# Second block: rotated queries summed in PSUM, key copies and sums of squares on the scalar engine

## The chip, the cores and the metric

One NeuronCore of one Trainium2 chip runs the whole program. The metric is device time in microseconds (us) of one execution; lower is better. The engines are named as in the profile: PE is TensorE (PEld its weight loads), DVE is VectorE, ACT is the scalar engine, POOL is GpSimd, and SP is the engine whose queue issues the large weight loads.

## What is computed

The program runs two transformer blocks over 256 tokens of width 1024. The first (gated linear attention, retention, a mixture of experts) is left alone by the change. The second is

```python
x = x + _hybrid_mixer(_rms_norm(x, norm1_g[l]), ...)
x = x + _memory_xattn(_rms_norm(x, norm2_g[l]), mem, ...)
x = x + _sq_relu_mlp(_rms_norm(x, norm3_g[l]), ...)
```

The mixer projects x once and makes from it three families of attention heads of width 64. The index queries `q_i` and the DSA queries `q_d` come from a normalized 256-wide row, the NSA queries `q_n` from x itself; each family has 8 heads, and each is rotated by position:

```python
x1, x2 = xf[..., :half], xf[..., half:]
return jnp.concatenate([x1 * cos - x2 * sin, x1 * sin + x2 * cos], axis=-1)
```

Keys are normalized over their 64 columns and rotated. The index scores choose for each token the 64 keys that DSA may see (a top-k), DSA and the three NSA branches are softmax attentions, and a fourth attention reads 256 memory rows through keys and values of 4 heads of width 128.

## The kernel before, in words

Activations are held transposed (features on the 128 partitions, tokens along the row) where they feed a product. A large product is done in two parts: each 128x1024 half of a weight tile is cast on ACT (`hi`, L285) and its rest is formed on DVE (`lo`, L287), both in `split`; then PE adds three products per piece (L299 to L301 in `w_step`, L312 to L314 in `x_step`). Weight tiles of 1 MB come by DMA on SP's queue (`load_w`, L277) into a ring of three buffers, and a load is issued when the last reader of its buffer, most often the `lo` of an earlier tile, is done. The projection weights of the mixer are the chunks 0 to 6 of `w3` (in the profile `wt<-w_in`): query and key rows first, chunk 3 and 4 for the key/value pairs `ks` and `kw`, chunk 5 and 6 for the NSA queries.

The order on each engine is not the order of the text: the framework's scheduler places the instructions of the second block, and each engine then works through its own queue strictly in that order. What stands behind a waiting instruction waits too.

The parts that the change touches lie in `second` and in the memory branch:

- `rope_T` (L1764) rotates two query banks of 128x512 in transposed form. ACT copies the projection from PSUM (`raw`, L1767), PE multiplies the copy with a permutation that swaps the halves of each head (`rot`, L1769), DVE multiplies the projection with the cosine table (L1771), the permuted one with the sine table (`rtmp`, L1773) and adds both (L1774). It is called for two banks each of the index queries (`Tqi`, banks `pq`), the DSA queries (`Tdsa_qn_g`) and, through `queries` (L1810), the NSA queries (`Tnsa_qn_g`, banks `pw`). `queries` also squares the banks on ACT (`sq`, L1817) and sums them by PE (`qss`, L1821); `fold` turns the sums into factors with a power on POOL (L355).
- `kT` (L1787) transposes keys on PE and copies them out on DVE (L1793): `Kki`, `Kkd`, `Kks`, `Kkw`.
- `knorm` (L1796) squares keys on ACT (`ksq`, L1799) and reduces the squares on DVE (`kss`, L1801).
- `memory_kv` (L1177) is a generator that is stepped from between the mixer's parts. Its `post` squares a bank of memory keys on ACT (L1197), reduces on DVE (`ks`, L1199), folds and scales on ACT (L1205); `turned` transposes the scaled keys on PE (`xkt`, L1212) and copies them on ACT (L1213). `kvm` (L1173) are the products that make memory keys and values.

Other names below: `ckT` the transposed 128-wide key row, `kvd` the DSA keys and values made from it, `cmp` the compressed keys, `ix` the index scores and the top-k on them (MAX8 and MATCH_REPLACE8), `sc` score banks, `mx` their row maxima on DVE (L2063), `sm` the exponentials on ACT (L2067), `sums` what follows them (L2069).

Of the kernel before, what the change touches and what calls it, by code (L numbers as in the profile page):

```python
# [13 lines left out]
AF = mybir.ActivationFunctionType  # L14
ALU = mybir.AluOpType
# [85 lines left out]
def prepare(inp):  # L101
# [119 lines left out]
    d = np.arange(128) % 64  # L221
    ang = (inv[d % 32][:, None] * np.arange(T, dtype=np.float32)[None, :]).astype(np.float32).astype(np.float64)
    ck.add('cosT', np.cos(ang))
    ck.add('sinT', np.sin(ang) * np.where(d < 32, -1.0, 1.0)[:, None])
    ck.add('perm', _rope_T()[2])
    ck.add('ropec', tab(16 * (p % 16) + 31))
    tri = np.where(p[None, :] <= p[:, None], 0.0, -1e30)
# [24 lines left out]
class Kern:  # L252
# [924 lines left out]
    def memory_kv(self, tiles):  # L1177
# [16 lines left out]

        def post(ps):
            sq = tiles("sq", F32)
            nc.scalar.activation(sq, ps, AF.Square)  # L1197
            s4 = S.tile([128, 2, 2], F32, tag="ks4", name="ks4")
            v.tensor_reduce(s4, sq.rearrange("p (t h d) -> p t h d", t=2, h=2), op=ALU.add, axis=AX.X)  # L1199
            f = self.fold(s4, 2, 128, r, r2, 1.0, "kf")  # L1200
            km = tiles("sq", F32)
            for t in range(2):
                for h in range(2):
                    cs = slice(t * 256 + h * 128, t * 256 + h * 128 + 128)
                    nc.scalar.mul(km[:, cs], ps[:, cs], f[:, t, h:h + 1])  # L1205
            return km
# [8 lines left out]
        km = post(self.k0)  # L1215
        yield
        pull(self.memory_keys(hf, self.load_w('wxkv', 1), "bg"), 99)
        turned(0, km)
        km = post(self.keys)
        yield  # L1220
        turned(1, km)
        yield

        for c in range(2):
# [442 lines left out]
    def second(self, P):  # L1667
        nc, I, v, S, x = self.nc, self.I, self.nc.vector, self.small, self.h

        def til(shape, tag, dt=F32, name=None, bufs=1):  # L1670
            return P.tile(shape, dt, tag=tag, name=name or tag, bufs=bufs)
# [14 lines left out]
        def cc(name):  # L1686
            a, n = self.at['const2'][name]
            return cst[:, a:a + n]
# [74 lines left out]

        def rope_T(ps, b, dst, cs, sn, tag):  # L1764

            raw = til(sq512, "s5", name="raw", bufs=5)
            nc.scalar.copy(raw, ps)  # L1767
            pr = self.bank("rot", "tp")
            nc.tensor.matmul(pr, lhsT=cc('perm'), rhs=raw, start=True, stop=True)  # L1769
            d, bc = dst[:, 2 * b:2 * b + 2, :], [128, 2, 256]  # L1770
            v.tensor_tensor(d, ps.rearrange("p (c q) -> p c q", c=2), cs[:, None, :].to_broadcast(bc), op=ALU.mult)  # L1771
            tmp = til([128, 2, 256], "s5", name="rtmp", bufs=5)
            v.tensor_tensor(tmp, pr.rearrange("p (c q) -> p c q", c=2), sn[:, None, :].to_broadcast(bc), op=ALU.mult)  # L1773
            v.tensor_tensor(d, d, tmp, op=ALU.add)  # L1774

        def rotate(dst, src, tab, shape, tag):

# [9 lines left out]
        def kT(src, nm, tag):  # L1787

            d = til([128, 256], "K" + nm)
            ps = self.bank("kT", "tp")  # L1790
            for t in range(2):
                nc.tensor.transpose(ps[:, t * 128:(t + 1) * 128], src[:, t].rearrange("p h d -> p (h d)"), self.ident)
            v.tensor_copy(d, ps[:, 0:256])  # L1793
            return d

        def knorm(kv, n, nm):  # L1796

            sq = til([128, 2, n, 64], "ksq")
            nc.scalar.activation(sq, kv, AF.Square)  # L1799
            ss = S.tile([128, 2 * n], F32, tag="kss%d" % n, name="kss")  # L1800
            v.tensor_reduce(ss, sq.rearrange("p t g d -> p (t g) d"), op=ALU.add, axis=AX.X)  # L1801
            rs = self.rstd(ss, 2 * n, 1.0 / 64, "krs%d" % n).rearrange("p (t g) -> p t g", t=2)
            kr = til([128, 2, n, 64], "kr")
            rotate(kr, kv, (tabs[nm][:, 0], tabs[nm][:, 1]), [2, n, 64], "swk2")
# [93 lines left out]
        for nm in ('dsa_qn_g', 'nsa_qn_g'):  # L1898
            tb = til([128, 2, 256], "tab" + nm)
            for o, src in enumerate(('cosT', 'sinT')):  # L1900
                nc.scalar.mul(tb[:, o], cc(src), self.sm(nm)[:, o:o + 1])
            tabs[nm] = tb

        pqd = qproj(0, "ps")
# [418 lines left out]
```

## Time and profile before

| | |
|---|---|
| median of 3 runs | 1072.5 us (1068.6 to 1072.56) |
| the profiled execution | 1070.49 us, its span 1068.7 us |
| PE busy | 1012.1 us, 95% of the span |
| DVE busy | 641.9 us, 60% |
| ACT busy | 449.1 us, 42% |
| POOL busy | 74.8 us, 7% |
| HBM read | 240.83 MB, 226 GB/s over the span |

Busy shares are means over the whole span, of which the changed part is a small piece; what a step is worth is read from its own stretch. A row of the timeline gives start, duration, engine, line, operation, output and inputs; in square brackets stands how long the engine was idle before, and what ended it. Neighbouring instructions overlap on PE, so its durations add up to more than the time that passes.

### The profile page before, as it was taken

What the parts mean: (1) busy time and instruction counts of PE and PEld (TensorE: products, weight loads), DVE (VectorE), ACT (ScalarE), POOL (GpSimd) and SP (SyncE); (2) the same over time, 40 slices, a digit from 0 to 9 for tenths busy, and PEclk for the clock granted to TensorE, in tenths of its full rate; (3) what the DMA queues carried; (4) which work ended last, traced back from release to release, by engine and by line L of the source; (5) the groups of instructions that cost most, each with busy time, mean ns of one, the idle gap of its engine ahead of it and who ended that gap; (6) DMA issues with size and microseconds to landing.
All of it is one profiled execution on the core that took longest, in us unless ns stands there. A gap on an engine that the chain in (4) does not pass through costs nothing.

```text
span 1068.7 us, 17877 instructions
## 1 busy us (share of the span) xinstructions
PE 1012.1 (95%) x7182; PEld 819.1 (77%) x7182; DVE 641.9 (60%) x1195; ACT 449.1 (42%) x785; POOL 74.8 (7%) x69
## 2 busy tenths in 40 slices
PE   5999998999999999999999878898999999999998
PEld 3889998998989999944444412687756889999997
DVE  4467879896565465634424312789776647555554
ACT  4356444333334634422222101685465646444442
POOL 0200001200131000000000000122100000000000
PEclk9999999999999999999999999999989999999999
DMA  9822654773327887888999999943311425555552
GB/s 357 313 73 79 241 193 158 178 277 111 118 83 284 320 350 274 246 309 322 387 420 420 420 421 421 383 158 120 119 40 40 159 82 194 189 182 186 193 197 79
DMA packets 36197, 243.07 MB, mean 227 GB/s; under 512 B 4032, under 2 KB 4432, under 8 KB 8464
## 3 DMA queue, kind: packets, MB, share of 16 engines
q1 hardware_dynamic: 34800, 236.53, 59.2%
q0 software_dynamic: 1312, 5.37, 1.5%
q8 instruction: 57, 0.93, 0.3%
q14 instruction: 28, 0.23, 0.1%
HBM read 240.83 MB, written 1.06 MB: 226 GB/s over the span
## 4 chain that ended last, share of the span: by engine, by line
PE 33%; DMA 12%; DVE 5%; ACT 2%; POOL 1%; issue 1%; SPq 0%; DVEq 0%; POOLq 0%; ACTq 0%
DMA wt<-wgu_in 7%; DMA wt<-wdn_in 4%; PE pw L299 3%; PE pw L300 3%; PE pw L301 3%; PE gu L1484 3%; PE acc L2292 3%; PE acc L2291 3%; PE acc L2293 3%; PE dn L1515 2%; DVE lo L287 1%; PE sc L1534 1%; POOL rstd L355 1%; DMA nfin<-nfin_in 1%; PE pT L2087 1%
## 5 line engine op out<-in xcount | busy, mean ns | idle before, releaser
L287 DVE TENSOR_TENSOR lo<-wt,hi 128x1024 fp32r<-128x1024 f32 x171 | 209.8, 1229 | 123.6 <-ACT hi L285 123.3
L285 ACT CAST hi<-wt 128x1024 fp32r<-128x1024 f32 x180 | 188.1, 1047 | 197.9 <-PE pw L300 113.2
L1484 PE MATMUL gu<-wt,XT 128*32 128x512 f32 (+1 forms) x608 | 92.2, 607 | 9.0 <-DMA wt<-wgu_in 8.9
L301 PE MATMUL pw<-fh,lo 128*128 128x256 f32 x352 | 98.2, 280 | 2.1 <-DVE lo L287 2.1
L300 PE MATMUL pw<-fl,hi 128*128 128x256 f32 x352 | 98.8, 281 | 1.1 <-DVE fl L371 1.1
L299 PE MATMUL pw<-fh,hi 128*128 128x256 f32 x352 | 98.5, 280 | 0.0
L1484 PEld LDWEIGHTS gu<-wt,XT 128*32 128x32 f32 (+1 forms) x608 | 23.3, 115 | 63.0 <-issue 43.7
L313 PE MATMUL px<-lo,h0h 128*128 128x256 f32 x240 | 68.6, 286 | 2.1 <-DVE lo L287 1.5
L301 PE MATMUL pw<-h0h,lo 128*128 128x256 f32 x240 | 68.1, 284 | 2.2 <-DVE lo L287 2.2
L312 PE MATMUL px<-hi,h0h 128*128 128x256 f32 x240 | 68.9, 287 | 0.0
L301 PEld LDWEIGHTS pw<-fh,lo 128*128 128x128 f32 x352 | 66.9, 190 | 2.4 <-DVE lo L287 2.4
L299 PE MATMUL pw<-h0h,hi 128*128 128x256 f32 x240 | 68.5, 285 | 0.1
L300 PE MATMUL pw<-h0l,hi 128*128 128x256 f32 x240 | 67.9, 283 | 0.0
L314 PE MATMUL px<-hi,h0l 128*128 128x256 f32 x240 | 67.9, 283 | 0.0
L300 PEld LDWEIGHTS pw<-fl,hi 128*128 128x128 f32 x352 | 66.1, 188 | 2.0 <-DVE fl L371 1.5
L299 PEld LDWEIGHTS pw<-fh,hi 128*128 128x128 f32 x352 | 66.1, 188 | 0.6
L1515 PE MATMUL dn<-wt,hT 128*32 128x512 f32 (+1 forms) x320 | 55.8, 596 | 4.9 <-DMA wt<-wdn_in 3.4
L1492 DVE TENSOR_TENSOR hid<-hid,gu 128x256 f32<-128x256 f32 x12 | 5.1, 421 | 78.6 <-ACT hid L1491 78.6
L2292 PE MATMUL acc<-lo,rh 128*128 128x512 f32 x128 | 49.8, 389 | 0.0
L2291 PE MATMUL acc<-hi,rh 128*128 128x512 f32 x128 | 49.8, 389 | 0.0
L2293 PE MATMUL acc<-hi,rlo 128*128 128x512 f32 x128 | 49.8, 389 | 0.0
L313 PEld LDWEIGHTS px<-lo,h0h 128*128 128x128 f32 x240 | 46.0, 192 | 3.3 <-DVE lo L287 2.0
(643 smaller groups left out, 2518.9 us busy)
## 6 DMA issues: line engine op xcount, KB each, us to landing
wt<-wgu_in SPq DMA_DIRECT2D x60, 1024.0 KB, 16.6
wt<-w_in SPq DMA_DIRECT2D x48, 1024.0 KB, 5.0
wt<-wdn_in SPq DMA_DIRECT2D x31, 1024.0 KB, 19.4
wt<-wada_in SPq DMA_DIRECT2D x16, 1024.0 KB, 5.3
wt<-wfi_in SPq DMA_DIRECT2D x16, 1024.0 KB, 4.8
wt<-wfo_in SPq DMA_DIRECT2D x16, 1024.0 KB, 4.8
wada<-wada_in SPq DMA_DIRECT2D x8, 1024.0 KB, 9.8
wt<-wxkv_in SPq DMA_DIRECT2D x4, 1024.0 KB, 6.4
```

Of the source, the lines that this page charges most:

```text
L285: nc.scalar.copy(hi, src)
L287: self.low = (engine or nc.vector).tensor_tensor(lo, src, hi.bitcast(F32), op=ALU.subtract).ins
L299: nc.tensor.matmul(o, lhsT=hi[:, c], rhs=xh[:, x, :], start=k == 0 and b == 0, stop=False)
L300: nc.tensor.matmul(o, lhsT=hi[:, c], rhs=xl[:, x, :], start=False, stop=False)
L301: nc.tensor.matmul(o, lhsT=lo[:, c], rhs=xh[:, x, :], start=False, stop=k == 7 and b == 1)
L312: nc.tensor.matmul(o, lhsT=xh[:, k, s], rhs=hi[:, c], start=k == 0 and t == 0, stop=False)
L313: nc.tensor.matmul(o, lhsT=xh[:, k, s], rhs=lo[:, c], start=False, stop=False)
L1484: return lambda: nc.tensor.matmul(pg[a:a + n, :], lhsT=XT[:, k, c:c + n], rhs=w[:, kk * 512:(kk + 1) * 512], start=k == 0, stop=k == 7)
L1515: return lambda: nc.tensor.matmul(pd[nh][a:a + m, :], lhsT=hT[:, kk, a:a + m], rhs=w[:, kk * 1024 + nh * 512:kk * 1024 + (nh + 1) * 512], ...
L2291: nc.tensor.matmul(a, lhsT=rh[:, k, s], rhs=whi[:, w], start=c == 0 and k == 0, stop=False)
L2292: nc.tensor.matmul(a, lhsT=rh[:, k, s], rhs=wlo[:, w], start=False, stop=False)
L2293: nc.tensor.matmul(a, lhsT=rlo[:, k, s], rhs=whi[:, w], start=False, stop=last)
```

## The change

`rope_T` now multiplies the projection on DVE with both tables, and PE sums the two results in one PSUM bank: the cosine part through the identity, the sine part through the permutation. ACT copies the sum out, where before it copied the input. The sine table changes its sign pattern, and both tables take the same gain column. `kT` copies on ACT. `knorm` and `post` square each head apart and let ACT's accumulator give the sum, so that DVE's reductions fall away. The memory keys of both halves are kept until the end and transposed together, behind the second half's products.

```diff
@@ -221,7 +221,7 @@
-    ck.add('sinT', np.sin(ang) * np.where(d < 32, -1.0, 1.0)[:, None])
+    ck.add('sinT', np.sin(ang) * np.where(d < 32, 1.0, -1.0)[:, None])
@@ -1194,9 +1194,11 @@
             sq = tiles("sq", F32)
-            nc.scalar.activation(sq, ps, AF.Square)
             s4 = S.tile([128, 2, 2], F32, tag="ks4", name="ks4")
-            v.tensor_reduce(s4, sq.rearrange("p (t h d) -> p t h d", t=2, h=2), op=ALU.add, axis=AX.X)
+            for t in range(2):
+                for h in range(2):
+                    cs = slice(t * 256 + h * 128, t * 256 + h * 128 + 128)
+                    nc.scalar.activation(sq[:, cs], ps[:, cs], AF.Square, accum_out=s4[:, t, h:h + 1])
@@ -1215,10 +1217,10 @@
         pull(self.memory_keys(hf, self.load_w('wxkv', 1), "bg"), 99)
-        turned(0, km)
-        km = post(self.keys)
+        km = km, post(self.keys)
         yield
-        turned(1, km)
+        for c in range(2):
+            turned(c, km[c])
@@ -1763,15 +1765,12 @@
         def rope_T(ps, b, dst, cs, sn, tag):
 
-            raw = til(sq512, "s5", name="raw", bufs=5)
-            nc.scalar.copy(raw, ps)
             pr = self.bank("rot", "tp")
-            nc.tensor.matmul(pr, lhsT=cc('perm'), rhs=raw, start=True, stop=True)
-            d, bc = dst[:, 2 * b:2 * b + 2, :], [128, 2, 256]
-            v.tensor_tensor(d, ps.rearrange("p (c q) -> p c q", c=2), cs[:, None, :].to_broadcast(bc), op=ALU.mult)
-            tmp = til([128, 2, 256], "s5", name="rtmp", bufs=5)
-            v.tensor_tensor(tmp, pr.rearrange("p (c q) -> p c q", c=2), sn[:, None, :].to_broadcast(bc), op=ALU.mult)
-            v.tensor_tensor(d, d, tmp, op=ALU.add)
+            for n, (tab, m) in enumerate(((cs, self.ident), (sn, cc('perm')))):
+                q = til([128, 2, 256], "s5", name="rtmp", bufs=5)
+                v.tensor_tensor(q, ps.rearrange("p (c q) -> p c q", c=2), tab[:, None, :].to_broadcast([128, 2, 256]), op=ALU.mult)
+                nc.tensor.matmul(pr, lhsT=m, rhs=q.rearrange("p c q -> p (c q)"), start=n == 0, stop=n == 1)
+            nc.scalar.copy(dst[:, 2 * b:2 * b + 2, :], pr.rearrange("p (c q) -> p c q", c=2))
@@ -1790,15 +1789,16 @@
-            v.tensor_copy(d, ps[:, 0:256])
+            nc.scalar.copy(d, ps[:, 0:256])
...
             sq = til([128, 2, n, 64], "ksq")
-            nc.scalar.activation(sq, kv, AF.Square)
             ss = S.tile([128, 2 * n], F32, tag="kss%d" % n, name="kss")
-            v.tensor_reduce(ss, sq.rearrange("p t g d -> p (t g) d"), op=ALU.add, axis=AX.X)
+            for t in range(2):
+                for g in range(n):
+                    nc.scalar.activation(sq[:, t, g], kv[:, t, g], AF.Square, accum_out=ss[:, t * n + g:t * n + g + 1])
@@ -1898,7 +1898,7 @@
-                nc.scalar.mul(tb[:, o], cc(src), self.sm(nm)[:, o:o + 1])
+                nc.scalar.mul(tb[:, o], cc(src), self.sm(nm)[:, 0:1])
```

What the scheduler makes of it is seen in the order of instructions. In the rows below, line numbers are those of the kernel that the rows belong to (after the change, the products with the tables are L1771, the products on PE L1772).

DVE at the first rotations, before (from the last step of the index keys to the `lo` of chunk 3's second half):

```order
L287 TENSOR_TENSOR lo<-wt,hi 128x1024
L1771 TENSOR_TENSOR Tqi<-pq,cst 128x512
L1773 TENSOR_TENSOR rtmp<-rot,cst 128x512
L1771 TENSOR_TENSOR Tqi<-pq,cst 128x512
L1774 TENSOR_TENSOR Tqi<-Tqi,rtmp 128x512
L1773 TENSOR_TENSOR rtmp<-rot,cst 128x512
L1774 TENSOR_TENSOR Tqi<-Tqi,rtmp 128x512
L1771 TENSOR_TENSOR Tdsa_qn_g<-pq,tabdsa_qn_g 128x512
L287 TENSOR_TENSOR lo<-wt,hi 128x1024
```

The same place after the change:

```order
L287 TENSOR_TENSOR lo<-wt,hi 128x1024
L1771 TENSOR_TENSOR rtmp<-pq,cst 128x512 x4
L1771 TENSOR_TENSOR rtmp<-pq,tabdsa_qn_g 128x512 x2
L388 TENSOR_REDUCE sst<-ssm 128x2
L354 TENSOR_SCALAR rstd<-sst 128x2
L1193 TENSOR_TENSOR rsm_7778<-rstd 128x2
L287 TENSOR_TENSOR lo<-wt,hi 128x1024
```

Both table products of the first DSA bank, and a small reduction for the memory rows, have come ahead of the second `lo`.

ACT from the DSA keys to the cast of chunk 4, before:

```order
L1910 ACTIVATE kvd<-kvd,fold 128x128 x2
L383 ACTIVATE junk,ssm<-wt 128x256
L1799 ACTIVATE ksq<-kvd 128x128
L383 ACTIVATE junk,ssm<-wt 128x256
L1817 ACTIVATE sq<-pq 128x512
L1767 COPY raw<-pq 128x512
L1817 ACTIVATE sq<-pq 128x512
L285 CAST hi<-wt 128x1024 x2
```

The same place after the change:

```order
L1910 ACTIVATE kvd<-kvd,fold 128x128 x2
L1801 ACTIVATE ksq,kss<-kvd 128x64 x2
L1817 ACTIVATE sq<-pq 128x512
L1773 COPY Tdsa_qn_g<-rot 128x512
L285 CAST hi<-wt 128x1024
L1817 ACTIVATE sq<-pq 128x512
L1773 COPY Tdsa_qn_g<-rot 128x512
L1792 COPY Kki<-kT 128x256
L1792 COPY Kkd<-kT 128x256
```

The cast of chunk 4's first half has come ahead of the squares of the second DSA bank.

DVE at the first score banks, before:

```order
L1773 TENSOR_TENSOR rtmp<-rot,tabnsa_qn_g 128x512
L2063 TENSOR_REDUCE mx<-sc 128x2
L1774 TENSOR_TENSOR Tnsa_qn_g<-Tnsa_qn_g,rtmp 128x512
L1771 TENSOR_TENSOR Tnsa_qn_g<-pw,tabnsa_qn_g 128x512
L2064 SCALAR_TENSOR_TENSOR mx<-mx,fp 128x2
L2063 TENSOR_REDUCE mx<-sc 128x2
L1644 TENSOR_TENSOR fold<-qss,q_7065 128x16
L354 TENSOR_SCALAR rstd<-fold 128x16
L1649 SCALAR_TENSOR_TENSOR fold<-rstd,r_7058 128x16
L1829 COPY fp<-fold 128x8 x2
L2063 TENSOR_REDUCE mx<-sc 128x2 x2
```

The same place after the change:

```order
L1771 TENSOR_TENSOR rtmp<-pw,tabnsa_qn_g 128x512 x2
L1646 TENSOR_TENSOR fold<-qss,q_7065 128x16
L354 TENSOR_SCALAR rstd<-fold 128x16
L1651 SCALAR_TENSOR_TENSOR fold<-rstd,r_7058 128x16
L1829 COPY fp<-fold 128x8 x2
L2063 TENSOR_REDUCE mx<-sc 128x2 x2
L2064 SCALAR_TENSOR_TENSOR mx<-mx,fp 128x2 x2
L2063 TENSOR_REDUCE mx<-sc 128x2 x2
```

All four maxima of the first scores now stand behind the fold of the NSA query sums.

## Rows read from the trace of the kernel before

**Rows 1.** The page, part 1: busy time, share of the span, instructions.

```profile
PE 1012.1 (95%) x7182; PEld 819.1 (77%) x7182; DVE 641.9 (60%) x1195; ACT 449.1 (42%) x785; POOL 74.8 (7%) x69
```

**Rows 2.** Windows: us, then busy us (instructions) of each engine, granted clock, DMA, GB/s.

```profile
704.55:712.34 7.79, 7.79 (x54) 6.83 (x55) 7.50 (x15) 6.70 (x20) 1.21 (x3) 1.00 0.41 135
712.34:721.86 9.52, 9.52 (x73) 8.38 (x71) 8.45 (x21) 5.31 (x13) 2.32 (x2) 1.00 0.61 223
721.86:742.37 20.51, 20.10 (x243) 17.99 (x242) 18.77 (x66) 12.40 (x26) 5.36 (x6) 1.00 0.30 104
742.37:759.65 17.28, 12.76 (x106) 12.17 (x107) 15.80 (x59) 7.06 (x14) 3.90 (x3) 1.00 0.51 183
759.65:766.90 7.25, 7.15 (x42) 4.91 (x41) 7.12 (x12) 3.78 (x8) 0.00 (x0) 1.00 0.38 145
766.90:774.40 7.50, 7.50 (x48) 5.78 (x48) 2.16 (x12) 3.89 (x14) 2.89 (x1) 1.00 0.00 0
```

**Rows 3.** Timeline of PE, 742 to 752 us: start, us, engine, line; idle before.

```profile
744.57 0.33 PE L1212 MATMUL xkt<-smalls,sq 128*128 128x128 f32 x1 [2.20 <-ACT sq L1205]
...
751.59 0.39 PE L301 MATMUL pw<-fh,lo 128*128 128x256 f32 x1 [2.06 <-DVE lo L287]
```

**Rows 4.** Chain of waits around 707 us: start, us on the chain.

```profile
707.32 0.86 PE rot L1769 x2
```

**Rows 5.** Timeline of PE, 706 to 713 us.

```profile
706.94 0.38 PE L1843 MATMUL ckT<-smalls,ms 128*128 128x128 f32 x2
...
711.73 0.61 PE L1907 MATMUL kvd<-wukv,ckT 128*128 128x128 f32 x4
```

**Rows 6.** Timeline of DVE, 706 to 709 us.

```profile
707.81 0.68 DVE L1771 TENSOR_TENSOR Tqi<-pq,cst 128x512 f32<-128x512 f32 x1
708.41 0.68 DVE L1773 TENSOR_TENSOR rtmp<-rot,cst 128x512 f32<-128x512 f32 x1
```

**Rows 7.** Timeline of DVE, SP queue and ACT, 712 to 719 us.

```profile
712.61 1.22 DVE L287 TENSOR_TENSOR lo<-wt,hi 128x1024 fp32r<-128x1024 f32 x1 [0.39 <-ACT hi L285]
...
713.86 0.33 SPq L277 DMA_DIRECT2D wt<-w_in  x1
...
717.08 0.60 ACT L1817 ACTIVATE sq<-pq 128x512 f32<-128x512 f32 x1 [2.02 <-DVE Tdsa_qn_g L1771]
...
718.80 2.00 ACT L285 CAST hi<-wt 128x1024 fp32r<-128x1024 f32 x2 [1.13 <-DMA wt<-w_in]
```

**Rows 8.** Groups of DVE instructions, 704 to 768 us: busy us, mean ns.

```profile
L1995 DVE MATCH_REPLACE8 ix<-m,ix 128x256 f32<-128x256 f32 (+1 forms) x16 | 5.4, 341 | 0.0
...
L1199 DVE TENSOR_REDUCE ks<-sq 128x4 f32<-128x512 f32 x2 | 1.3, 668 | 0.0
...
L1793 DVE COPY Kks<-kT 128x256 f32<-128x256 f32 x1 | 0.4, 425 | 0.0
```

**Rows 9.** Timeline of ACT, 728 to 737 us.

```profile
728.29 0.25 ACT L2007 ACTIVATE sqc<-kvc 128x64 f32<-128x64 f32 x1
...
736.72 0.42 ACT L1799 ACTIVATE ksq<-kvkw 128x256 f32<-128x256 f32 x1
```

**Rows 10.** Timeline of DVE, POOL and ACT, 766 to 775 us.

```profile
766.88 0.17 DVE L1644 TENSOR_TENSOR fold<-qss,q 128x16 f32<-128x16 f32 x1
...
767.34 2.89 POOL L355 TENSOR_TENSOR rstd<-rstd,mhalf 128x16 f32<-128x16 f32 x1 [13.54 <-DVE rstd L354]
...
770.63 1.28 DVE L2063 TENSOR_REDUCE mx<-sc 128x2 f32<-128x512 f32 x2
...
772.07 0.56 ACT L2067 ACTIVATE sm<-sc,mx,fp 128x256 f32<-128x256 f32 x1 [3.58 <-DVE mx L2064]
...
774.40 0.17 DVE L2069 TENSOR_SCALAR sums<-sums 128x8 f32<-128x8 f32 x1 [2.29 <-ACT sm L2067]
```

**Rows 11.** Windows around the stretch at the lower clock (PEclk).

```profile
778.00:781.00 3.00, 1.55 (x7) 0.51 (x5) 2.06 (x5) 3.00 (x14) 0.00 (x0) 1.00 0.68 284
781.00:787.60 6.60, 6.21 (x17) 3.13 (x19) 3.46 (x14) 3.58 (x12) 0.00 (x0) 0.50 0.01 2
```

## The prediction

> **What bounds the kernel now.** I read the page first: TensorE (PE) is busy 95% of the span [rows 1], so a change is worth what it does to PE's idle time and to PE's own work. The changed lines run in one stretch, from 704 to about 775 us, so I cut that stretch into windows [rows 2]. The reader is to see that PE is busy without a gap until 721.86, and all but 0.4 us until 742.37, while VectorE (DVE) is busy 89 to 96% in the same windows. From 742.37 to 759.65 PE is busy only 12.76 of 17.28 us: 4.5 us idle. PE's timeline names the two longest waits there [rows 3]: 2.20 us for the scaled memory keys (their transposes stand ahead of the query projection, and the scaling waits for DVE's reduction among its top-k passes), and 2.06 us for a split's low part, also late on DVE. Then the bound changes: in 766.90 to 774.40 DVE is busy 2.16 of 7.50 us and PE is filled with memory products, but the chain of the first scores decides the end (below).
>
> So there are two purses. DVE's relief can buy at most PE's idle time: 0.4 + 4.5 + 0.1 us [rows 2] up to 766.9. PE's new work is paid in full wherever PE has no gap.
>
> **The change, part by part.**
>
> *Rotation, work on PE.* One product of 128x512 in f32 takes 0.86 us on the chain of waits [rows 4]; it shows as two pieces. Six rotations had one product each; each gets a second one, with the identity. That is 6 x 0.86 = 5.2 us more on PE. It exceeds the 5.0 us of idle time just counted, so even perfect cover leaves about +0.2.
>
> *Rotation, order on DVE and PE (index queries).* Before, the permutation product needed only a scalar copy and ran at once behind the ckT transposes at 706.94 [rows 5], while the split on DVE was still going. Now it needs DVE's products with the tables, and those stand behind that split, which hands over at 707.81; they then start 0.60 us apart [rows 6]. So PE, ready at about 707.2, has its first operand near 708.5: a wait of 1.3 us. Four products follow where two were: +1.7. The kv products (kvd), at 711.73 before [rows 5], move by +3.0.
>
> *Index, DSA queries.* Two more products: +1.7 on a PE without gaps, sum +4.7. DVE meanwhile is stuck: its queue now has both products for the first DSA bank ahead of the next split. Between the transposes at 707.2 and 711.73 PE ran two rotations (1.72 us) and 24 projection products, so 0.12 us each [rows 4, 5]; now these begin after four products, at 712.0, and the first bank is full 12 products later, at 713.4. DVE has nothing to do from 710.2 to 713.4, and the split behind starts near 715.75 (two products 1.2, then a small reduction with its power on GpSimd, some 1.1) where it started at 712.61 [rows 7]. That is 3.1 late, and something hangs on it: the SP queue issued the next weight load (w3 chunk 4) at 713.86, right when this split had read its buffer; the load ended the wait of the scalar engine (ACT) at 718.80, 4.9 later [rows 7]. Now the load comes near 717.0 and lands near 721.9. In ACT's new order this chunk's cast stands ahead of the squares of the second DSA bank, which ran at 717.08 before it [rows 7]. These squares wait for load and cast (1.0) and end near 723.5; PE comes to the sums behind them at about 720.8. Wait: 2.7 us. It takes the place of the 0.4 that PE lost before. At 742.37 of the old clock PE is now at +4.7 + 2.7 - 0.4 = +7.0. The bounds of this wait are 0 (load on time) and 2.7; I take 2.7 because every step has a row.
>
> *Sums of squares and key copies on ACT.* DVE loses two reductions of 0.67, four copies of 0.42 and three smaller reductions [rows 8], and of the rotation one in three passes (18 become 12, at 0.60 apart: 3.6). In all about 7 us. ACT gets accumulating squares instead of plain ones: a 64-wide one takes 0.25 and a 256-wide plain one 0.42 [rows 9], so four for one cost 0.6 to 1.3 us more each time (the upper end with the read of the accumulator, bounded by one more such instruction without overlap), under 5 us over five places, and the four copies 0.4 each. ACT was busy 7.06 of 17.28 and 12.40 of 20.51 us [rows 2]: covered by its idle time except where it stands in front of a chain; the index scores wait some 0.5 of it on DVE, inside what DVE saves. The sign in the sine table and the table column [0:1] cost nothing: same instructions. No DMA changes place on the SP queue; GpSimd does the same powers, some in another order, at 7% load.
>
> *Memory keys turned later.* The first keys' four transposes leave the place where PE waited 2.20 us and go, with the others, behind the last rotation. So the 96 products of the NSA query projection follow the memory products directly. DVE's relief lets the first low part be ready. The next three still come between top-k passes: a split of 1.22 [rows 7] and some nine small passes, the larger ones 0.34 [rows 8], take DVE an estimated 3.4 us per half chunk, PE's 24 products take 2.9. I take a wait of 0.55 three times, 1.65 in all; bounds 0 and the 4.5 of before. The stretch shrinks by 4.5 - 1.65 and by 0.8 of transposes and mask products that move behind it: -3.7. At the NSA rotation (759.65) PE stands at +3.3. This is the part that pays.
>
> *NSA rotation and scores.* DVE does the last two table products only behind three splits, so PE waits about 1.5 us for them with two more products to run; old and new paths differ by 0.4. The fold of the query sums, at 766.88 [rows 10], goes to about +3.6. Behind it GpSimd's power takes 2.89. Before, DVE had reduced one pair of score banks ahead of the fold, so ACT worked on four heads under that wait and started the other four at 772.07, ending before DVE's 774.40 [rows 10]. Now all four reductions stand behind the fold. ACT starts at about 772.07 + 3.3 with eight heads at 0.54 (four took 2.2 of those 2.33 us), and the second pair of banks comes after six memory products on PE. That adds 2.3 (bounds 0 if PE's later products made the early reductions late anyway, and 2.9, the wait itself).
>
> **Sum:** 3.0 + 1.7 + 2.7 - 0.4 - 3.7 + 0.3 + 2.3 = +5.9 us. The profiled execution took 1070.49 us (span 1068.7), so **1076.4 us**. The median of the three runs, 1072.5, lies 2.0 above that execution; against it the forecast is +0.4%, and with the sum set on the median it would be 1078.4, +0.55%. I call 0.5% (5.4 us) what a measurement can tell from no change; this case straddles it.
>
> **Rivals.**
>
> *Not slower: the relief of DVE reaches the chain.* If chunk 4's load is not late, the 2.7 goes; if DVE, ahead by part of its 7 us, also has the low parts ready, 1.65 more goes: 1072.0. It decides at the split of 712.61: if DVE starts it before 713.5, the load lands before ACT needs it. For it: DVE is busy over 89% up to 742 and stands in both waits of rows 3. Against it: the new order itself, where that split is behind products that PE cannot feed earlier. Its floor: no idle left (+5.2 - 5.0 = +0.2), the late scores without cost: 1070.7. Faster than that needs PE's clock.
>
> *The clock falls once more.* The granted clock went to 0.50 (the lower level, 1.2 GHz) from 781.0 to 787.6, after three microseconds in which PE worked 1.55 of 3.00 [rows 11]; it did not fall in 742 to 760 [rows 2]. The new waits of 1.3 and 2.7 us near 707 and 721 are such gaps. One more stretch like it, 6.6 us at half speed, costs 3.3: 1079.7. The Trainium skill ("TensorE: Matmul & The Clock Gate", Part 1) says that a monitor sets PE's clock by how busy PE has been, so a gap can halve it. By that rule the time here would be 1079.7; the rows above show one gap that did it and two waits of over 2 us that did not, so it has less than an even chance.
>
> *The clock does not fall at 781*, because the memory products last longer there: 1076.4 - 3.3 = 1073.1. The scores keep their shape, so I give it little.
>
> *The change does not do what it says:* excluded by the order of instructions, where DVE has 23 rows fewer.
>
> **Numbers.** The forecast case 0.52, with its own range 1074 to 1079; DVE's relief 0.27; clock falls 0.13; no fall 0.05; 0.03 for the rest, a gain over 5.4 us among it. Lower end of the range 1068.5, two below the floor of the first rival for the spread of runs (1068.6 to 1072.56); upper end 1082.5, where 4.5 of idle stays instead of 1.65 (+2.9, to 1079.3) or the clock falls and one of the two comes with it. Slower by over 0.5% (above 1077.9): a bit over half of the forecast case and nearly all of the clock's: 0.41. Faster (under 1067.1): 0.05. Within: 0.54.
>
> **What would show it.** Right: idle PE before the first rotation product (about 1.3) and before the second set of DSA sums (about 2.7, with ACT's cast waiting for the load of w_in); the load issued near 717; no wait for the key transposes near 742; first scores' exponentials eight in a row behind GpSimd's power. Wrong: the load at 714, or PE's idle time in the stretch under 2 us in all (then the first rival), or a second stretch at half clock.

## The result, and the profile after

The changed kernel takes 1081.88 us (median of 4 runs, 1078.4 to 1084.93), the kernel before beside it 1071.62 (4 runs, 1068.6 to 1072.56): a ratio of 1.0096, 95% interval 1.0072 to 1.0119. It is slower, by some 10 us. The profiled execution took 1080.9 us, 10.4 more than that of before.

The page of the changed kernel, span and part 1 (answers to rows 1):

```profile
span 1079.1 us, 17932 instructions
...
PE 1022.4 (95%) x7194; PEld 826.2 (77%) x7194; DVE 633.5 (59%) x1180; ACT 453.9 (42%) x820; POOL 73.6 (7%) x69
```

DVE is 8.4 us less busy and PE 10.3 us more, of which the added products explain 5.2. To find the place of the loss, compare the same instruction in both traces:

| instruction on PE | before, us | after, us | apart |
|---|---|---|---|
| `pq` product after the first wait for a low part | 704.55 | 708.96 | 4.4 |
| `kT` transposes of the selected keys | 735.08 | 745.06 | 10.0 |
| `vbd`, last step before the NSA rotation | 759.54 | 766.12 | 6.6 |
| second mask product `sc<-cmr` | 776.98 | 790.43 | 13.5 |
| score product at 800.20 of before | 800.20 | 810.22 | 10.0 |
| a product near the end | 1041.78 | 1052.18 | 10.4 |

So 4.4 us were lost before the first changed instruction runs, 6.0 in and just behind the changed stretch. Windows of the changed kernel (us, then busy us and instructions of each engine, granted clock, DMA, GB/s) show where the first part comes from; the two below answer to the same stretches of before, which follow:

```profile
21.35:28.15 6.80, 5.89 (x28) 5.44 (x32) 3.06 (x4) 3.05 (x5) 0.20 (x1) 0.50 1.00 401
106.70:110.05 3.35, 3.35 (x18) 3.35 (x18) 0.00 (x0) 0.63 (x1) 0.00 (x0) 0.50 0.72 286
```

```profile
21.35:28.15 6.80, 6.54 (x51) 4.75 (x51) 3.21 (x4) 2.51 (x5) 0.00 (x0) 1.00 1.00 393
106.70:110.05 3.35, 3.35 (x30) 3.35 (x29) 3.35 (x4) 1.15 (x2) 0.00 (x0) 1.00 0.45 110
```

The clock was granted at half (0.50, 1.2 GHz) in two stretches that ran at full speed in before, and PE got through 28 and 18 products where before it did 51 and 30. No instruction there was changed. The first experiment asks whether that belongs to the change.

In the changed stretch, PE's timeline (start, us, engine, line; idle before) has these waits, which answer to rows 3:

```profile
712.95 0.70 PE L1772 MATMUL rot<-rtmp,smalls 128*128 128x512 f32 x1 [1.25 <-DVE rtmp L1771]
...
756.10 0.38 PE L301 MATMUL pw<-fh,lo 128*128 128x256 f32 x1 [0.69 <-DVE lo L287]
759.48 0.38 PE L301 MATMUL pw<-fh,lo 128*128 128x256 f32 x1 [0.37 <-DVE lo L287]
763.08 0.38 PE L301 MATMUL pw<-fh,lo 128*128 128x256 f32 x1 [0.61 <-DVE lo L287]
769.80 0.35 PE L1821 MATMUL qss<-smalls,sq 128*128 128x2 f32 x2 [1.69 <-ACT hi L285]
```

The wait for the first rotation's operand is there (1.25); the waits for scaled keys and low part of rows 3 are gone, and three short ones stand in their place. New is 1.69 us before the NSA sums. Then come the two windows that answer to rows 11, where the clock falls 2.5 us after that wait, and not, as before, at 781:

```profile
772.30:775.65 3.35, 3.35 (x6) 1.29 (x5) 0.28 (x1) 0.60 (x1) 0.00 (x0) 0.50 0.41 174
775.70:790.00 14.30, 14.30 (x90) 11.21 (x89) 6.54 (x23) 6.58 (x20) 2.90 (x1) 1.00 0.00 1
```

The last rows are of the DSA path that the forecast spoke of: the cast of chunk 4 and the squares behind it on ACT, PE's sums, then the last reader of each of the two ring buffers (ACT's memory squares, DVE's split) and the two loads on the SP queue (answers to rows 7):

```profile
723.30 1.05 ACT L285 CAST hi<-wt 128x1024 fp32r<-128x1024 f32 x1 [1.02 <-DMA wt<-w_in]
724.26 0.59 ACT L1817 ACTIVATE sq<-pq 128x512 f32<-128x512 f32 x1
...
725.49 0.95 PE L1821 MATMUL qss<-smalls,sq 128*128 128x2 f32 x8
...
718.04 0.19 ACT L383 ACTIVATION_READ_ACCUMULATOR junk<-wt 128x1 f32 x1
...
720.56 1.23 DVE L287 TENSOR_TENSOR lo<-wt,hi 128x1024 fp32r<-128x1024 f32 x1
...
718.25 0.33 SPq L277 DMA_DIRECT2D wt<-w_in  x1
721.81 0.33 SPq L277 DMA_DIRECT2D wt<-wxkv_in  x1
```

The cast waits 1.02 us for the load, but PE reaches the sums without a wait: the squares end at 724.85.

### The profile page after: what moved, and what is told of

It reads as the page before. It is cut to its first block, busy times and chain, and to the rows that moved or that the text cites. A ratio compares the mean times of both kernels' runs of the same rounds, so it can differ in the third digit from the quotient of the medians.

```text
span 1079.1 us, 17932 instructions
## 1 busy us (share of the span) xinstructions
PE 1022.4 (95%) x7194; PEld 826.2 (77%) x7194; DVE 633.5 (59%) x1180; ACT 453.9 (42%) x820; POOL 73.6 (7%) x69
## 4 chain that ended last, share of the span: by engine, by line
PE 36%; DMA 11%; DVE 4%; ACT 2%; issue 1%; POOL 1%; SPq 0%; DVEq 0%; ACTq 0%; POOLq 0%
DMA wt<-wgu_in 7%; DMA wt<-wdn_in 4%; PE pw L299 3%; PE pw L301 3%; PE pw L300 3%; PE gu L1486 3%; PE acc L2293 3%; PE acc L2291 3%; PE acc L2292 3%; PE dn L1517 2%; PE sc L1536 1%; DVE lo L287 1%; PE gat L1444 1%; PE sc L2057 1%; PE rot L1772 1%; PE pT L2087 1%
## 5 line engine op out<-in xcount | busy, mean ns | idle before, releaser
L301 PEld LDWEIGHTS pw<-h0h,lo 128*128 128x128 f32 x240 | 47.2, 197 | 2.5 <-DVE lo L287 2.4
```

Of the source, the lines that this page charges most:

```text
L301: nc.tensor.matmul(o, lhsT=lo[:, c], rhs=xh[:, x, :], start=False, stop=k == 7 and b == 1)
```

## The experiments

Twelve kernels ran, each timed beside the kernel before. One table holds the results. "Clock share" is span x (1 - mean granted clock) of each execution, averaged: the time that the half clock can have cost at most, since PE's idle time counts in it too. "Remainder" is the mean time less that. For before (68 executions beside the experiments) the standard error of the remainder is 0.2 us, for the others 0.4 to 1.3; that of their clock share 0.5 to 1.8. A profile shows one execution of several: those of e9 and e10 are the ones with the smallest clock share of their kernels (3.2). The remainder also holds what lies behind PE's last product: from its start to the end of the span it is 5.5 us in the profiles of e3, e6, e10 and e11, and 4.3 in the other ten. Whether that belongs to these kernels or to the execution is open.

| kernel | runs | ratio (95% interval) | mean us | clock share | remainder |
|---|---|---|---|---|---|
| before | 68 | 1 | 1071.8 | 8.3 | 1063.5 |
| e1 before again | 12 | 1.0007 (0.9992 to 1.0022) | 1072.4 | 8.7 | 1063.6 |
| changed kernel, first runs | 4 | 1.0096 (1.0072 to 1.0119) | 1081.8 | 10.5 | 1071.2 |
| e2 changed kernel again | 6 | 1.0081 (1.0056 to 1.0106) | 1081.1 | 9.7 | 1071.4 |
| e3 rotation undone | 6 | 1.0059 (1.0038 to 1.0081) | 1077.7 | 12.6 | 1065.2 |
| e4 rotation alone | 6 | 1.0073 (1.0054 to 1.0091) | 1080.2 | 8.8 | 1071.4 |
| e5 keys later alone | 12 | 1.0023 (1.0008 to 1.0038) | 1074.4 | 10.8 | 1063.5 |
| e6 scalar moves alone | 6 | 1.0051 (1.0034 to 1.0067) | 1076.6 | 11.5 | 1065.1 |
| e7 no identity products | 5 | 1.0085 (1.0072 to 1.0098) | 1080.1 | 12.1 | 1068.0 |
| e8 top-k later | 6 | 1.0044 (1.0031 to 1.0057) | 1076.6 | 13.3 | 1063.4 |
| e9 top-k later, rotation undone | 12 | 1.0014 (1.0000 to 1.0028) | 1073.0 | 7.9 | 1065.0 |
| e10 two waits out | 6 | 1.0063 (1.0042 to 1.0085) | 1078.7 | 7.5 | 1071.2 |
| e11 order mended | 6 | 1.0064 (1.0049 to 1.0079) | 1079.5 | 7.0 | 1072.5 |
| e12 top-k later, memory squares | 12 | 1.0017 (1.0002 to 1.0032) | 1074.0 | 10.7 | 1063.3 |

**Both kernels again.** No edit.

> The kernel before, once more, beside itself. Between the two profiled executions the changed stretch (704 to 800 us of before) accounts for +5.6 us and the first 110 us, where no instruction differs, for +4.4 us: there the granted clock of the changed kernel was 0.50 for 6.8 us at 21.3 and for 3.4 us at 106.7, and in before it was 1.00. Theory A (these early falls come by chance to either kernel): the ratio is 1.000 within 0.003, and the granted clocks of this kernel's executions spread from about 0.995 down to 0.988, as those of the changed kernel did. Rival B (the early falls belong to the changed program): all executions of this kernel have a clock of 0.993 or more, and none falls before 600 us in the profile.

> The changed kernel, once more. Theory A: in the changed stretch the same +5.6 us, early falls in some executions and not in others; the ratio is between 1.005 and 1.009, and executions with a clock of 0.994 take 1076 to 1079 us. Rival B: a fall near 21 us in this profile too, all clocks at 0.993 or less, ratio 1.0096 or more.

A window of e1, the kernel before:

```profile
21.15:27.90 6.75, 6.25 (x28) 5.47 (x32) 2.65 (x4) 2.89 (x5) 0.00 (x0) 0.50 1.01 416
```

The same early fall, 28 products in 6.75 us, in the kernel before; e2, the changed kernel, had a shorter one (3.4 us at 21.8). So the early falls come to either kernel, in some executions and not in others, and rival B falls. What the change itself costs is better read from all ten of its executions: mean 1081.4 against 1071.8, of which 7.8 in the remainder (1071.3 against 1063.5) and 1.7 in the clock share (10.0, standard error 1.2, against 8.3), which is no certain difference.

**The parts apart.** e3 puts the old rotation back into the changed kernel, e4 puts the new one alone into the kernel before: the hunks of the change on `rope_T`, the sine table and the gain column, backwards and forwards.

```diff
-            for n, (tab, m) in enumerate(((cs, self.ident), (sn, cc('perm')))):
...
+            nc.tensor.matmul(pr, lhsT=cc('perm'), rhs=raw, start=True, stop=True)
```

> The changed kernel with the old rotation (scalar copy, one permutation product, three passes of VectorE; old sign and column of the sine table), keeping squares and key copies on the scalar engine and the memory keys turned later. Theory A (the loss is the six identity products, 6 x 0.86 = 5.2 us, the 1.25 us wait for the first operand and the 1.69 us wait of the NSA sums behind a cast; the keys turned later pay 2.5 to 3.4): 6 to 8 us less than the changed kernel, a ratio of 0.995 to 0.999 to before. Rival C (the squares and copies on the scalar engine cost: they stand in front of casts and exponentials): ratio over 1.002, and waits of PE on ACT's casts or squares stay.

> The kernel before with the new rotation alone (squares, key copies and memory keys as before). Theory A: +5.2 us of products and +1.3 us of wait for the first operand; the waits of before for the scaled keys (2.20) and the low part (2.06) shrink by 0 to 2 as VectorE has one pass in three fewer: ratio 1.004 to 1.007. Rival C: under 1.003, since then the rest of the change carries the loss.

e4 carries the whole loss: its remainder is that of the changed kernel (1071.4), and rival C falls for it. Its waits did not shrink as expected, though; others took their place, 2.27 us for a rectification at 738.53, 0.84 for a low part and 2.41 for a bank at 771.84:

```profile
771.84 0.35 PE L1818 MATMUL qss<-smalls,sq 128*128 128x2 f32 x2 [2.41 <-DVE kcT L2024]
```

Undoing the rotation (e3) takes 6.2 us off the remainder; the clock share is 2.5 higher (standard error 1.5). So e3 is 3.7 us faster than the changed kernel where theory A expected 6 to 8, and its ratio (1.0059) lies where rival C had it. One row of e3's PE timeline and two of its windows show how:

```profile
747.64 0.69 PE L1794 MATMUL kT<-smalls,k 128*128 128x128 f32 x2 [4.09 <-DVE k L1810]
...
746.45:753.20 6.75, 5.56 (x19) 4.26 (x20) 6.08 (x20) 0.38 (x1) 1.92 (x1) 0.50 0.36 117
753.30:775.00 21.70, 21.70 (x150) 18.42 (x149) 15.09 (x37) 10.63 (x22) 2.89 (x1) 1.00 0.35 122
```

With the scaled keys out of its way PE comes early to the window keys, waits 4.09 us for them (DVE makes them among its top-k passes), and the clock falls in that wait.

e5 and e6 take the other two parts alone, e5 the hunk of `memory_kv` that turns the keys later, e6 those of `post`, `knorm` and `kT`:

```diff
-        turned(0, km)
-        km = post(self.keys)
+        km = km, post(self.keys)
```

```diff
-            v.tensor_copy(d, ps[:, 0:256])
+            nc.scalar.copy(d, ps[:, 0:256])
...
-            nc.scalar.activation(sq, kv, AF.Square)
+                    nc.scalar.activation(sq[:, t, g], kv[:, t, g], AF.Square, accum_out=ss[:, t * n + g:t * n + g + 1])
```

> The kernel before with the memory keys turned later, and nothing else. In the run with the rotation undone the time saved came back as one wait of 4.09 us for the key product of VectorE, which stands among its top-k passes at 747.5 us. Theory V (VectorE's queue up to about 748 us decides when TensorE can go on; what arrives earlier waits there): the 2.46 us of waits for the scaled keys go, and the waits for the window keys and the low part that follow grow by about as much; the sum of TensorE's waits from 735 to 765 us stays at 4 to 5 us, ratio 0.998 to 1.004, with a clock fall near 746 in some executions as in before. Rival D (the turned keys pay by themselves, as the forecast had it): waits of 2 us or less there, ratio 0.996 to 0.998.

> The kernel before with the squares with accumulation and the key copies on the scalar engine, and nothing else. Theory V: VectorE loses some 3.5 us of work ahead of 751, so the waits of 2.46 and 2.06 us shrink by 1 to 3 us together: ratio 0.997 to 1.000. Rival C (these moves cost, since their squares stand in front of casts on the scalar engine): ratio over 1.002 and new waits of TensorE on scalar casts or squares.

e5 went as theory V has it: the 2.46 us of waits for the keys came back as this one, the waits from 735 to 765 sum to 3.9 us (4 to 5 expected), and the remainder did not move. Its 2.6 us over before lie in the clock share (10.8 against 8.3).

```profile
751.60 0.44 PE L1792 MATMUL kT<-smalls,k 128*128 128x128 f32 x2 [2.72 <-DVE k L1807]
```

e6 cost 1.6 us in the remainder and 3.2 in the clock share, against theory V and with rival C's ratio. Its ACT timeline, and the PE row that waits behind it (0.41 us in the same place of before):

```profile
727.03 0.25 ACT L1804 ACTIVATE ksq<-kvks 128x64 f32<-128x64 f32 x1
727.17 0.20 ACT L1804 ACTIVATION_READ_ACCUMULATOR ksq<-kvks 128x1 f32 x1
...
727.98 0.90 ACT L1188 ACTIVATE hf<-wt,smalls 128x256 f32<-128x256 f32 x2
728.78 0.58 ACT L1979 ACTIVATE rl<-ix 128x512 f32<-128x512 f32 x1
...
729.42 0.37 PE L1975 MATMUL ix<-Kki,Tqi 64*128 64x128 f32 x1 [1.10 <-ACT rl L1979]
```

Four squares with their accumulator reads take 0.95 us (727.03 to 727.98) where one took 0.42 [rows 9], and the rectification that frees a score bank stands behind them. e3 and e9, which have the same moves, have 1.7 and 1.5 us. The row explains 0.7 of the 1.6 us. Where the rest lies is not shown: from the first instruction compared above (704.55 in before) to the last product the profile of e6 takes as long as that of before (356.5 us in both, with half-clock stretches counted at half), and 1.2 us more lie behind the last product.

**The products priced.** e7 leaves the identity products out of the changed kernel, so its rotated queries hold the sine part alone.

```diff
-                nc.tensor.matmul(pr, lhsT=m, rhs=q.rearrange("p c q -> p (c q)"), start=n == 0, stop=n == 1)
+                if n:
+                    nc.tensor.matmul(pr, lhsT=m, rhs=q.rearrange("p c q -> p (c q)"), start=True, stop=True)
```

> The changed kernel without its six identity products: the cosine products of VectorE are still made but not summed, so the rotated queries hold only the sine part. It prices the products. Forecast's term (six products at 0.86, all paid): 5.2 us less than the changed kernel. Theory V: the four ahead of the top-k passes (3.4 us) are partly paid back as waits for VectorE near 745 to 760, only the two of the NSA queries (1.7) are paid in full, so 1.7 to 4 us less than the changed kernel, with waits of 3 to 5 us from 735 to 765 where it had 1.67.

The time is nearly the same as with them (1080.1 against 1081.4), short of both expectations; the remainder is 3.3 us less (standard error 1.4), the clock share 2.0 more. So of the 5.2 of the forecast's term some 3.3 came off the remainder. PE's waits tell where the rest went: the first rotation waits 1.74 us (1.25 in the changed kernel), and 4.5 us stand at both ends of the stretch that theory V named, where the changed kernel has 3.4, but behind ACT's rectifications and before the sums, not for low parts:

```profile
735.73 0.38 PE L312 MATMUL px<-hi,fh 128*128 128x256 f32 x1 [2.06 <-ACT rl L1977]
...
765.43 0.47 PE L1822 MATMUL qss<-smalls,sq 128*128 128x2 f32 x3 [2.43 <-ACT Tnsa_qn_g L1774]
```

All idle times of PE over 0.15 us, from behind the first instruction compared above (704.55 in before) to the last product, sum to 9.5 us here and 7.9 in the changed kernel, so 1.6 of the 5.2 came back, which leaves 3.6.

**Order on DVE.** e8 writes the top-k passes of the kernel before behind the NSA query projection; e9 does so in e3's kernel.

```diff
-            for rd in range(8):
+            picks.append((t, ac, n, m0))
...
+        for t, ac, n, m0 in picks:
+            for rd in range(8):
```

> The kernel before with the code of the top-k passes written behind the NSA query projection, which puts two of VectorE's low parts and the window keys ahead of most passes; the work is the same. Theory V (the order on VectorE, not its load, makes TensorE's waits at 744.6 and 751.6): most of the 4.5 us of waits go, and the passes fill VectorE where it is idle later (766 to 774): 2 to 4 us less, ratio 0.996 to 0.998, no clock fall near 746. Rival (VectorE's load is the limit: it is busy to 758 whatever the order): the waits come back at the NSA rotation or at the mask products, ratio 0.999 to 1.001.

> The kernel with the rotation undone, and the top-k passes written behind the NSA query projection as in the run before. So far the mean granted clock, times the span, says how the loss splits: before loses 8 us of its span to the half clock; the runs with the keys later, with the scalar moves, with the rotation undone and with the top-k passes later lose 11 to 13 us, each with a wait of TensorE of 2.0 to 4.1 us and a half-clock stretch that begins within 3 us of that wait. Theory W (in this stretch one wait of about 2 us or more also costs a stretch at half clock): here the scalar engine no longer stands before the casts waiting for VectorE's reduction, so the wait of 1.99 us for a cast goes; with no wait over 1.7 us from 735 to 775 the clock's loss returns to about 8 us and the time is 1068 to 1072, ratio 0.997 to 1.001. If the longest wait stays at 2 us or more, the loss stays at 11 us or more and the ratio is over 1.002. Rival (the loss of clock does not hang on waits): loss of 11 to 13 us without such a wait.

In e8 both waits of rows 3 are gone, but at 757.3 PE waits 1.99 us for a cast and then 1.07 for a low part, for ACT stood before its casts waiting for what DVE makes of the second memory keys:

```profile
755.17 1.14 ACT L1205 ACTIVATE sq<-kvm,fold 128x128 f32<-128x128 f32 x4 [7.25 <-DVE fold L1649]
```

The remainder is unchanged, the clock share 5 us up: PE ran at half clock from 758.3 (3.4 us), 768.6 (10.2) and 792.4 (3.4). The forecast of 2 to 4 us less was wrong. In e9 ACT still waits there, 6.54 us for the same fold, and PE still waits for the cast behind it, but less: 1.36 us, then 0.94 for a low part. These are ACT's row, PE's longest wait from 735 to 800, the window with the one fall there, and a window behind:

```profile
751.22 1.14 ACT L1207 ACTIVATE sq<-kvm,fold 128x128 f32<-128x128 f32 x4 [6.54 <-DVE fold L1651]
...
753.35 0.39 PE L299 MATMUL pw<-fh,hi 128*128 128x256 f32 x1 [1.36 <-ACT hi L285]
...
754.25:757.60 3.35, 2.80 (x13) 2.80 (x14) 3.21 (x11) 1.42 (x2) 0.00 (x0) 0.50 0.53 161
...
775.00:795.00 20.00, 18.70 (x102) 10.66 (x99) 13.91 (x45) 12.57 (x43) 0.00 (x0) 1.00 0.14 53
```

e3 and e9 do the same work in another order, on DVE first of all (some products and casts moved with it on PE and ACT). The remainder is the same (1065.2 and 1065.0), and the clock share falls from 12.6 to 7.9 us, with the wait of 4.09 us gone. That is the share that theory W had forecast for e9, though the ratio (1.0014) came out a little over the range given, and the wait for the cast did not go but got shorter. The 4.6 us are not the price of the wait of 4.09 alone: e3's profile has a second fall of 6.8 us, at 783.9, behind waits of 1.20 and 0.63 us; that of e9 has waits of 0.66 and 0.64 there and no fall.

**The waits of the change taken out.** e10 queues a later low part on DVE behind the first rotation's table products, and writes the compressed keys' transpose and copy (`kbT`, `kcT`, `vbd`) ahead of the NSA query projection. e11 has the first edit, and e8's order of the passes.

```diff
+            pw = [self.split(wk[:, 0:1024], after=(None, None if i else turned_q))]
-            pb, = self.proj_x('w3', 3 + i, [(hi, lo)])
+            pb, = self.proj_x('w3', 3 + i, [(hi, lo)], wt=wk, parts=pw)
```

```diff
+        pt = self.bank("kbT", "bg")
...
         pqn = []
...
-        pt = self.bank("kbT", "bg")
```

> The changed kernel with two orders mended and the same work: the low part of a later weight chunk is queued on VectorE behind the first rotation's table products (it stood ahead of them, and TensorE waited 1.25 us), and the compressed keys' transpose and copy are written ahead of the NSA query projection (their copy stood behind two low parts, and the NSA sums waited 1.69 us for its bank). By the sum alone: 2.9 us less than the changed kernel. Theory W: the half clock that began at 772.3 and 769.4 us in its two profiles, behind the second wait, gets shorter or goes, and 1.7 to 5 us more are saved: 3 to 7 us less in all, ratio 1.002 to 1.006 to before. Rival (VectorE's load makes the waits come back elsewhere): within 1.5 us of the changed kernel.

> The changed kernel, with the top-k passes written behind the NSA query projection and the later low part queued behind the first rotation's table products; the work is the same. The 1.25 us of wait before the first rotation and the three low-part waits (1.67 together) should go; the NSA sums may still wait about 1 us for the copy of the compressed keys, which stands behind the passes. If the six identity products are the rest of the price (5.2 us of TensorE's work with no wait left to pay for it): 2 to 5 us less than the changed kernel and still 4 to 6 us over before, ratio 1.0035 to 1.006, clock's loss near 8 us if no wait reaches 2 us. Rival (waits and clock were the price, the products are covered): ratio under 1.003.

Both waits went in e10, but `vbd` now came so early that it waited for DVE's copy of the compressed keys:

```profile
753.56 0.38 PE L2027 MATMUL vbd<-kb,cst 128*128 128x128 f32 x1 [4.38 <-DVE kcT L2025]
```

The remainder did not move (1071.2); 2.7 us less in the mean (3 to 7 were expected) nearly all lie in the clock share, and a fall of 3.4 us stands right behind the new wait (754.0), none from 757 to 795. That also limits theory W: a wait of 4.38 us, and the share stayed at 7.5; e4, with waits of 2.27 and 2.41, has 8.8. In e11 (1.9 us less than the changed kernel) the waits are 1.21, 1.21 and 1.55; the clock share is the lowest of all (7.0), the ratio 1.0064, a little over the range given, and the remainder still 9 us above that of before. The rival (waits and clock as the price) would have been under 1.003. The edit did not take all waits out, so the ratio alone does not settle it; the sum of waits does: counted as for e7, PE's idle times sum to 7.6 us in e11 and e10, 7.9 in the changed kernel and 8.7 in before (7.2 in e1). The slower kernels do not wait longer, so the rival falls, and the price lies for the most part in what PE runs.

**A version that might beat both.** e12 is the kernel before with keys later, the memory keys' squares alone on ACT, and e8's order: the hunks shown above, of e6 only that of `post`.

> The kernel before with three things: memory keys turned later, the memory keys' sums of squares on the scalar engine, top-k passes written behind the NSA query projection. Key norms, key copies and the rotation stay as before. Against the run with the passes later and the rotation undone, the key norms' squares and the copies no longer stand in front of the index scores' rectifications (TensorE waited 1.10 us there, 0.41 before), so 1 to 1.5 us come back; no wait over 1.7 us, clock's loss near 8 us: 1069.5 to 1072, ratio 0.998 to 1.001. Rival (VectorE, with some 3 us of reductions and copies back, hands over the low parts late again): a wait of 2 us or more, loss of 11 us, ratio over 1.002.

The remainder is that of before, but a cast made PE wait 2.76 us, and the share is 10.7: the rival's outcome, but for the ratio (1.0017, where it had over 1.002). Since the memory keys' squares on ACT are in it, what e6's moves cost belongs to the others, the key norms' squares and the key copies. No kernel of the study is faster than before.

## Why the prediction was right and wrong

The forecast was 1076.4, +5.9 on the profiled execution, with 0.54 on no measurable change and 0.41 on slower by over 0.5%. Measured: +10.3 in the first runs, +9.6 over all ten, so it came out in the 0.41; the direction of the likeliest case was right, its size about 60% of what was measured. 1081.88 lies inside the range, but above that case's own (1074 to 1079), and neither way in which the forecast reached its upper end was seen: the 4.5 us of idle time did not stay, and the profile has no further fall in the changed stretch. The profile lost 6.0 us in and just behind the changed stretch, close to the 5.9, and that is luck: two terms of 2.7 and 2.3 us did not occur, one of 0.3 came out at 3.4, and over all executions 7.8 us in the remainder stand against the 5.9.

- **First rotations and DSA queries (forecast +4.7 without the load's wait): right, 0.9 short.** The wait was 1.25 us where 1.3 was said, and the four second products came 0.86 to 0.96 behind the first ones. From 704.55 to 735.08 of before the distance grew by 5.6.
- **Late load, 2.7 us: wrong.** The step that failed is "this split had read its buffer". The `w_in` load did not wait for that split any more: in the new order it took the ring buffer that ACT's memory squares read last (they ended at 718.23, the load went out at 718.25), and the `wxkv` load took the split's (which ended at 721.79; the load went out at 721.81). It came 3.2 us before the time forecast (717.0, or 721.4 on the clock of after). The split itself was about as late as forecast: 720.56, where 715.75 is 720.2 on the clock of after.
- **Keys later and DVE's relief, -3.7: right in this kernel, wrong as a gain of that part.** From 735.08 to 759.54 the distance shrank by 3.4, and three waits of 0.69, 0.37 and 0.61 sum to 1.67 where 1.65 was said. But e5 shows no gain in the remainder by itself. The likely reading is that PE must be late for the passes' results to be ready, and that in the changed kernel the rotation's products make it late, so that the gain is a discount on their price. No run shows it: e4, which turns the keys as before, has the remainder of the changed kernel.
- **ACT's added work covered: wrong in e3, e6 and e9.** The term was nothing; these three measure 1.5 to 1.7 us in the remainder. The step took ACT's busy share for its cover, but the squares stand in one queue in front of rectifications that free score banks, which shows as 0.7 us of added wait; the rest was not assigned. In the changed kernel itself this place shows 0.30 us of wait, less than the 0.41 of before, and what the moves cost there was not measured.
- **NSA rotation, +0.3: the largest miss.** Two products more (1.7) found no gap to hide in, and the sums waited 1.69 us: 3.4. The row names ACT's cast, which ended only as PE went on; e4, e8, e9 and e11 name DVE's copy `kcT` in the same wait, and e10, which moves that copy, has no wait there. Its DVE row in the changed kernel:

```profile
767.19 2.36 DVE L287 TENSOR_TENSOR lo<-wt,hi 128x1024 fp32r<-128x1024 f32 x2
769.47 0.18 DVE L2027 COPY kcT<-kbT 128x32 f32<-128x32 f32 x1
```

  The forecast had looked for the table products behind the splits, not for a small copy that empties the bank the sums need.
- **Late scores, +2.3: did not happen.** The four maxima stand behind the fold as forecast, but PE's waits for the exponentials are 0.37 and 0.64 where before had 1.20 and 0.64: all 32 memory products stood behind the last rotation, from 778.84 on, where before had begun them at 762.85, and they filled the time, so the lower bound (0) was nearer.
- **Clock.** The rival "falls once more" was given 0.13 and 3.3 us. In the profile the fall near 781 was replaced by a shorter one at 772.3, and e2 had one of 13.7 us from 769.4. Over all executions the share rose by 1.7, which cannot be told from chance here. What can be told is that kernels with the same work in another order lie 4.6 (e3, e9) and 5.0 us (e8, before) apart in the share, while the forecast treated it as one event with one price. The Trainium skill ("TensorE: Matmul & The Clock Gate", Terms) puts the penalty of a reduced clock at the throttled time x (1 - its ratio), by which a stretch of 6.8 us costs an estimated 3.4. The traces show less: from 779.63 to 789.83, across the fall at 781, before took 10.20 us, and e9, which has no fall there, 7.60 for the same products, so 2.6. Before had also waited 0.4 us inside the fall.
- **Work on DVE.** The profile counts 15 instructions fewer (1195 to 1180), where the forecast spoke of 23 rows fewer.

What stays open: of the 7.8 us that the change adds to the remainder, and the rotation alone as much, the six products account for 5.2 of PE's work. The first wait of 1.25 is no further part of it, since PE's waits as a whole did not grow (8.7 and 7.2 us in the two profiles of before, 7.9 and 7.8 in those of the changed kernel). Some 2.6 us were not assigned, and e10 and e11 show that taking single waits out does not bring them back. Whether the share's rise in the changed kernel is its own was not settled either.

## What to carry to other kernels

Relief of a busy engine is worth what the bottleneck waits for it, and that wait must be followed to the next thing which the relieved engine makes: here each wait taken out (e3, e5, e8, e10) stood again a few microseconds on, at keys, a cast or a copy. Work added to an engine that is 95% busy is paid for whatever it saves elsewhere: here 5.2 us of products came with 7.8 us in all, and leaving them out gave back some 3.3 of these. Where effects are under 1%, read the granted clock of every execution and split it off before comparing parts: two kernels with the same work (e3, e9) lay 4.8 us apart, 4.6 of them in the clock share.

## What was not expected of the hardware

In all fourteen profiles each half-clock stretch between 735 and 795 us began inside a wait of TensorE or within 3 us behind one of 0.6 us or more. Not every wait was followed by one: the waits of 2.20 and 2.06 us in before [rows 3] were not, and the 4.38 us of e10 cost one fall of 3.4 us. The same program had falls near 21 and 105 us in some executions and none in others. Nor did a busy engine end a fall at once. In e2 this window ran at half clock from end to end, with PE busy throughout (few products, since the f32 products of 128x512 took about twice as long: 1.87 us from the first of the rotation to the second, where 0.86 to 0.96 stand at full clock):

```profile
769.40:783.00 13.60, 13.60 (x36) 7.93 (x35) 3.82 (x12) 3.40 (x7) 2.89 (x1) 0.50 0.16 69
```

No price of a wait in clock comes out of these runs: the kernel with a wait of 4.09 us (e3) has a share of 12.6 us, that with one of 4.38 (e10) has 7.5, and the highest share (e8, 13.3) goes with a longest wait of 1.99. What an order costs in clock has to be read over many executions of it.
